# Streams' states loaded ahead into the ring for unsplit weights, and the first MLP pair's differences formed in the mixer's last round

## The chip, the cores and the metric

One core of a Trainium2 chip runs the whole kernel. The metric is device time in microseconds (us), lower is better. The core's engines are TensorE (PE in the rows; PEld is its loading of stationary operands), VectorE (DVE), ScalarE (ACT), GpSimd (POOL) and SyncE (SP), which here issues every DMA, in the order of its queue.

## The reference, cut to what matters

One inference step of one layer, in fp32, for a prompt of 16 meta and 2048 tokens and for 8 running streams of 16 new tokens each, width 1024.

```python
q, k, v, gate, ga, gb = split(rms_norm(x, g_pre) @ w_in)     # 1024 -> 3072
q, k = rope(q), rope(k) * HEAD_DIM ** -0.5                   # 4 heads of 128
scores = einsum('bihd,bjhd->bhij', q, k) * d_intra           # retention, chunks of 64
out    = scores @ v + (q @ S) * d_in                         # S: carried state, 128 x 128
S_new  = S * exp(lg * L) + einsum('bjhd,bjhe,hj->bhde', k, v, d_out)
ret    = group_norm(out) * silu(gate)
conv   = silu(layer_norm(depthwise_conv31(ga * sigmoid(gb))))
x = x + rms_norm(concat(ret, conv) @ w_out)
x = x + rms_norm(square(relu(rms_norm(x) @ w_mlp_in)) @ w_mlp_out)
```

For a running stream S is an input (`state_ret`, 8 streams x 4 heads x 128 x 128) and S_new an output (`o_ss` in the kernel).

## The kernel before, in words

Tokens lie along the free axis, features along the 128 partitions. Each fp32 product is made of three matmuls: both operands are split into a high and a low part, and `mm3` adds low x high, high x low and high x high (L514 to L516). A split is one ScalarE copy and one subtraction on DVE or POOL (L383, L384).

**Mixer.** The tokens form six groups of 2 or 3 blocks of 128 (`LAY`); group `SG` = 3 holds two prompt blocks and one block with the 8 streams. For each group in turn the projection `w_in`, four heads (`head`, names `tk`, `up`, `us`, `os`, `ob`, `ot`), the convolution with its norm (`conv_norm`, names `cv`, `mu`, `z`, `acc`, `cacc`, `st`, `rb`) and the output projection `w_out` (result `yo`, stored in `yscr`) run as generators that are advanced between the main matmuls `mm`. Weights are read unsplit once (`raw`, a ring of 5 tiles of 128x512 in the mixer, `RB`), split, stored to DRAM (`wkeep_in`, `wkeep_out`) and from then on read as `whi` and `wlo` through a ring of nine. The normalized mixer output of all groups is stored in DRAM in pieces of 128 rows (`hd`).

**Sampled streams.** In group 3 each head goes through the 8 streams two at a time: load of two states into `sst` (a ring of two tiles, L1038), product with the masked queries (`os`, L1040), decay and addition of the new outer products `us` in place (DVE, L1042), store to `o_ss` (L1044).

**Column sums.** `rstd_bcast` (L487) sums the squares over the partitions: for each block of 128 tokens the squares are the stationary operand and a 128x128 tile of ones is the moving one; only column 0 of the result is read. A call leaves two records in the profile.

**MLP.** The columns are taken in three groups `G` of two halves (384, 384 and 320 columns each). For each, seven products replace eight in the manner of Strassen, so seven combined operands `P1` to `P7` (names `op`) are made of the four quarters of `hd`: with b11, b12 the two column halves of the upper rows and b21, b22 of the lower, the operands are b11, b21, b22 and the differences b12 - b11 (P5), b22 - P5 (P6), b22 - b12 (P7) and b21 - P6 (P4). For G = 1 and 2 `differences` forms the four on POOL while the MLP of the pair before runs, stores them in `td`, and `reload` brings them in and splits them. For G = 0 `make_h2` does it on DVE after the mixer's last head, while TensorE still makes the last `w_out` products: it loads a 128x768 piece with both halves (`st`, L616), subtracts (L622) and splits (L384). Layer 2's seven products (`SEVEN`, `plan`) are the same in both kernels.

The order within each engine is settled when the program is built, by a scheduler that plays the program through; SyncE's queue is in that order too.

Of the kernel before, what the change touches and what calls it, by code (L numbers as in the profile page):

```python
# [12 lines left out]
F32 = mybir.dt.float32  # L13
# [3 lines left out]
ALU = mybir.AluOpType  # L17
# [3 lines left out]
P = 128  # L21
D_MODEL, SEQ, N_META, PAST_LEN = 1024, 2048, 16, 512
NS, SL = 8, 16
# [146 lines left out]
def build(nc, T):  # L170
    lg = _log_gamma()
    with tile.TileContext(nc, schedule_with_timeline_sim=True) as tc, ExitStack() as top:
# [306 lines left out]
        def rstd_bcast(acc, W, n):  # L479
# [6 lines left out]
            for b, s in enumerate(starts):  # L486
                nc.tensor.matmul(ps[:, b, :], acc[:, s:s + P], ones, start=True, stop=True)  # L487
# [108 lines left out]
        OPS = (P1, P2, P6, P5, P7, P3, P4)  # L596
# [3 lines left out]
        td = [None] + [dram.tile([4, 4, P, n], F32, name=f"td{n}") for n in NH2[1:]]  # L600
# [6 lines left out]

        def make_h2(G, which, eng, put):

            n = NH2[G]  # L610
            need = {P1: (0,), P2: (1,), P3: (1,), P5: (0,), P6: (0, 1), P7: (0, 1), P4: (0, 1)}
            for k in range(4):
                bs = {}
                for r in sorted({r for x in which for r in need[x]}):
                    t = st_tile()[:, :2 * n]
                    nc.sync.dma_start(t, hd[G][k + 4 * r])  # L616
                    bs[r, 0], bs[r, 1] = t[:, :n], t[:, n:]
                yield

                def diff(a, b):  # L620
                    t = s_tile(n)
                    eng.tensor_tensor(out=t, in0=a, in1=b, op=ALU.subtract)  # L622
                    return t

                parts = {P1: bs.get((0, 0)), P2: bs.get((1, 0)), P3: bs.get((1, 1))}
                if {P4, P5, P6} & set(which):
                    parts[P5] = diff(bs[0, 1], bs[0, 0])
                if {P4, P6} & set(which):
                    parts[P6] = diff(bs[1, 1], parts[P5])
                for x in which:  # L630
                    if x == P7:
                        parts[x] = diff(bs[1, 1], bs[0, 1])
                    if x == P4:
                        parts[x] = diff(bs[1, 0], parts[P6])
                    yield from put(x, k, parts[x])

        def put_home(G, eng):
            def put(x, k, part):
                t = hops[G, x] if k else home(G, x)
                split(part, t[:, k], t[:, 4 + k], eng)  # L640
                if k == 3:
                    h2_made.add((G, x))
                yield
            return put

        def differences(G):

            n = NH2[G]
            for k in range(4):
# [7 lines left out]
                for i in range(4):  # L657
# [5 lines left out]
                    ts.append(t)  # L663
                    yield
# [294 lines left out]
        def head_tail(gi, h, kr, qr, vf):  # L959
# [4 lines left out]
            sblk = slice(nb * P, N)  # L964

# [58 lines left out]
            if smp:  # L1024
                osm = auxp.tile([P, 512], F32, tag="aux", name="os")[:, :P]
                for s0 in range(0, NS, 4):
# [8 lines left out]
                    for s1 in (0, 2):  # L1035
                        s = s0 + s1
                        sst = tp.tile([P, 2, P], F32, tag="sst", name="sst", bufs=2)
                        nc.sync.dma_start(sst, T["state"][h][:, s:s + 2, :])  # L1038
                        for i in range(2):
                            nc.tensor.matmul(osm, qdm[:, (s + i) * (P - SL):(s + i) * (P - SL) + P], sst[:, i],  # L1040
                                             start=(s + i == 0), stop=False)
                        nc.vector.scalar_tensor_tensor(out=sst, in0=sst, scalar=float(np.exp(lg[h] * SL)),  # L1042
                                                       in1=us[:, s1:s1 + 2], op0=ALU.mult, op1=ALU.add)
                        nc.sync.dma_start(T["o_ss"][h][:, s:s + 2, :], sst)  # L1044
# [54 lines left out]
        for gi in range(len(LAY)):  # L1099
# [24 lines left out]
            if gi == LAST:  # L1124
                rate["norm"] = 2
            for h, t in late(gi):
                head_unit(gi, h, t)
# [354 lines left out]
```

## Time and profile before

| | |
|---|---|
| median of 3 runs | 2417.91 us (2410.08 to 2423.68) |
| profiled execution | 2409.09 us |
| its span | 2407.3 us |
| mean granted clock of TensorE | 0.987 |

The span is the time from the first to the last recorded instruction, the profiled execution the device's time for the same run. The granted clock is a share of full speed: 1 means 2.4 GHz all along.

### The profile page before, as it was taken

The page shows a single profiled execution, that of the slowest core. Times are in us where ns is not written, and L with a number is a line of the kernel's source. Part 1 is how long each engine was busy: PE and PEld are TensorE (multiplying, and loading weights), DVE is VectorE, ACT ScalarE, POOL GpSimd, SP SyncE. Part 2 cuts the span into 40 slices and gives each one's busy share as a digit, 9 for nine tenths or more (in the row PEclk, how much of TensorE's full clock was granted, in tenths as well). Part 3 has the DMA queues.
Part 4 walks back from the last instruction along what each step waited for, and adds up shares of the span by engine and source line. Part 5 has one row for each costly group of instructions (what it writes and reads, how often), then busy time and mean ns, then how long its engine had stood idle before and what let it go on. Part 6 is the DMA issues. An engine that isn't in the chain of part 4 may idle for free. (4 is left out here: it accounts for less than half of the span.)

```text
span 2407.3 us, 41425 instructions
## 1 busy us (share of the span) xinstructions
PE 2312.4 (96%) x14250; PEld 2277.5 (95%) x14250; DVE 1708.5 (71%) x3704; ACT 1005.1 (42%) x2240; POOL 1470.6 (61%) x1532
## 2 busy tenths in 40 slices
PE   8898999998899998999999999999899999999997
PEld 7898999998899998999999999999899999999997
DVE  8999897896997965546543347678776676666666
ACT  5534334123223133544434445344444443444442
POOL 6847232131133113978888776687897747888874
PEclk9999999999999999999999999999999999999998
DMA  8887787897688778858896557676765567565562
GB/s 316 284 313 273 269 291 265 243 329 275 204 275 285 242 251 322 281 203 291 279 321 228 188 203 253 229 237 216 259 215 166 167 222 260 181 203 175 190 216 95
DMA packets 246338, 584.55 MB, mean 243 GB/s; under 512 B 31984, under 2 KB 106480, under 8 KB 246128
## 3 DMA queue, kind: packets, MB, share of 16 engines
q1 hardware_dynamic: 246128, 581.92, 71.2%
q8 instruction: 112, 1.84, 0.3%
q14 instruction: 98, 0.80, 0.1%
HBM read 445.20 MB, written 136.61 MB: 242 GB/s over the span
## 5 line engine op out<-in xcount | busy, mean ns | idle before, releaser
L1227 PE MATMUL mm<-op,wp 128*128 128x384 f32 (+1 forms) x1344 | 441.9, 329 | 13.3 <-DMA wp<-wprod 12.7
L1229 PE MATMUL mm<-op,wp 128*128 128x384 f32 (+1 forms) x1344 | 439.3, 327 | 1.5 <-POOL wp L322 1.5
L1228 PE MATMUL mm<-op,wp 128*128 128x384 f32 (+1 forms) x1344 | 439.8, 327 | 0.0
L835 DVE SCALAR_TENSOR_TENSOR cv<-ext,par,cv 128x384 f32<-128x384 f32 (+1 forms) x720 | 381.8, 571 | 2.0
L514 PE MATMUL mm<-hhi,whi 128*128 128x384 f32 (+2 forms) x992 | 332.6, 336 | 17.4 <-ACT hhi L731 5.4
L516 PE MATMUL mm<-hhi,wlo 128*128 128x384 f32 (+2 forms) x992 | 331.9, 336 | 7.3 <-DMA wlo<-wkeep_in 3.1
L515 PE MATMUL mm<-hlo,whi 128*128 128x384 f32 (+2 forms) x992 | 331.3, 334 | 0.3
L283 POOL TENSOR_TENSOR wlo<-raw,whi 128x512 fp32r<-128x512 f32 x180 | 239.0, 1347 | 127.2 <-ACT whi L282 52.2
L1320 DVE TENSOR_TENSOR ya<-l2y,ya 128x384 f32<-128x384 f32 (+1 forms) x384 | 194.6, 519 | 117.1 <-PE l2y L1317 116.3
L1227 PEld LDWEIGHTS mm<-op,wp 128*128 128x128 f32 x1344 | 252.9, 188 | 21.8 <-DMA wp<-wprod 7.8
L1229 PEld LDWEIGHTS mm<-op,wp 128*128 128x128 f32 x1344 | 252.9, 188 | 1.9 <-POOL wp L322 1.7
L1228 PEld LDWEIGHTS mm<-op,wp 128*128 128x128 f32 x1344 | 253.0, 188 | 0.1
L356 POOL TENSOR_TENSOR wq<-raw,wq 128x256 fp32r<-128x256 f32 x240 | 183.1, 776 | 58.7 <-ACT wq L355 58.0
L514 PEld LDWEIGHTS mm<-hhi,whi 128*128 128x128 f32 x992 | 191.5, 193 | 19.8 <-ACT hhi L731 5.6
L384 POOL TENSOR_TENSOR fo<-c,fo 128x384 fp32r<-128x384 f32 (+1 forms) x168 | 166.2, 990 | 65.3 <-ACT fo L383 64.1
L516 PEld LDWEIGHTS mm<-hhi,wlo 128*128 128x128 f32 x992 | 190.7, 193 | 10.2 <-DMA wlo<-wkeep_in 3.8
L515 PEld LDWEIGHTS mm<-hlo,whi 128*128 128x128 f32 x992 | 191.0, 193 | 1.5 <-DVE hlo L732 1.1
L1320 DVE TENSOR_TENSOR ya<-l2w,ya 128x384 f32<-128x384 f32 (+1 forms) x288 | 143.1, 517 | 19.3 <-PE l2w L1317 16.7
L1241 DVE TENSOR_TENSOR c<-mm,sn 128x384 f32<-128x384 f32 (+1 forms) x144 | 76.5, 532 | 112.7 <-PE mm L1229 74.5
L322 POOL TENSOR_TENSOR wp<-raw,wp 128x512 fp32r<-128x512 f32 x96 | 126.9, 1327 | 43.9 <-ACT wp L321 31.5
L882 POOL TENSOR_TENSOR sw<-sw,sin 128x384 f32<-128x384 f32 (+2 forms) x48 | 48.3, 1006 | 171.0 <-ACT sw L879 168.5
L282 ACT ACTIVATE whi<-raw 128x512 fp32r<-128x512 f32 x192 | 112.9, 623 | 85.4 <-DMA raw<-w_in 19.0
(261 smaller groups left out, 6292.2 us busy)
## 6 DMA issues: line engine op xcount, KB each, us to landing
wp<-wprod SPq DMA_DIRECT2D x224, 512.0 KB, 3.9
raw<-w SPq DMA_DIRECT2D x256, 256.0 KB, 3.8
wprod<-wp SPq DMA_DIRECT2D x112, 512.0 KB, 3.9
whi<-wkeep_in SPq DMA_DIRECT2D x108, 512.0 KB, 6.2
wlo<-wkeep_in SPq DMA_DIRECT2D x108, 512.0 KB, 5.3
raw<-w_in SPq DMA_DIRECT2D x72, 256.0 KB, 5.6
whi<-wkeep_out SPq DMA_DIRECT2D x36, 512.0 KB, 6.0
wlo<-wkeep_out SPq DMA_DIRECT2D x36, 512.0 KB, 5.7
```

Of the source, the lines that this page charges most:

```text
L283: (nc.vector if i < 24 and i % 4 == 0 else nc.gpsimd).tensor_tensor(out=lo[:, c], in0=raw, in1=hi[:, c].bitcast(F32), op=ALU.subtract)
L322: tt(out=op[:, H:], in0=src, in1=op[:, :H].bitcast(F32), op=ALU.subtract)
L356: nc.gpsimd.tensor_tensor(out=op[:, o + H:o + 2 * H], in0=src, in1=op[:, o:o + H].bitcast(F32), op=ALU.subtract)
L384: (eng or nc.gpsimd).tensor_tensor(out=lo, in0=src, in1=hi.bitcast(F32), op=ALU.subtract)
L514: nc.tensor.matmul(ps, whi(k), ahi(k), start=(k == 0), stop=False)
L515: nc.tensor.matmul(ps, whi(k), alo(k), start=False, stop=False)
L516: nc.tensor.matmul(ps, wlo(k), ahi(k), start=False, stop=(k == nk - 1))
L835: nc.vector.scalar_tensor_tensor(out=o, in0=src(t), scalar=wt, in1=o, op0=ALU.mult, op1=ALU.add)
L1227: nc.tensor.matmul(ps, hi, ops[:, k, :n], start=start, stop=False, skip_group_check=not first)
L1228: nc.tensor.matmul(ps, hi, ops[:, 4 + k, :n], start=False, stop=False, skip_group_check=not first)
L1229: nc.tensor.matmul(ps, lo, ops[:, k, :n], start=False, stop=(k == 3), skip_group_check=not first)
L1320: last_y[0] = nc.vector.tensor_tensor(out=y, in0=ps, in1=y, op=ALU.add)
```

## The change

It consists of three edits. The states of a head's eight streams are loaded at the beginning of `head`, four streams at a time, into tiles of the `raw` ring, and are used from there; product, update and store take four streams in one go. The column sums use one column of the ones. The four differences of G = 0 are formed on POOL by a new generator `first_differences`, queued behind `mlp_in` in the last round of the mixer, with pieces of `hd` loaded into the two halves of one tile `df`; they are stored in a `td` of their own, and `make_h2` gives way to `reload`, which `differences` of G = 1 and 2 already use. (`reload` loads a k pair, 128x2x384, of one operand, from `hd` for P1, P2, P3 and from `td` for the others, and splits it, half on DVE and half on POOL for G = 0.)

```diff
--- before.py
+++ after.py
@@ -484,7 +484,7 @@
             nb = len(starts)
             ps = auxp.tile([P, 4, P], F32, tag="aux", name="st")
             for b, s in enumerate(starts):
-                nc.tensor.matmul(ps[:, b, :], acc[:, s:s + P], ones, start=True, stop=True)
+                nc.tensor.matmul(ps[:, b, :1], acc[:, s:s + P], ones[:, :1], start=True, stop=True)
             y = rsqrt_small(ps[:, :nb, 0], nb, n)
             dg = spool.tile([P, NM // P, P], F32, tag="dg", name="dg", bufs=1)
             for b in range(nb):
@@ -593,55 +593,16 @@
                 yield
 
 
-        OPS = (P1, P2, P6, P5, P7, P3, P4)
         HOME = {P1: "hhi", P2: "hlo", P6: "chi", P5: "clo", P7: "x", P3: "hhi", P4: "hlo"}
         hops, h2_made = {}, set()
 
-        td = [None] + [dram.tile([4, 4, P, n], F32, name=f"td{n}") for n in NH2[1:]]
+        td = [dram.tile([4, 4, P, n], F32, name=f"td{G}") for G, n in enumerate(NH2)]
 
         def home(G, x):
             pool = {"h": hp, "c": catp, "x": xp}[HOME[x][0]]
             t = pool.tile([P, 8, NM if pool is catp else WM], F32R, tag=HOME[x], name=f"op{x}")
             hops[G, x] = t[:, :, :NH2[G]]
             return hops[G, x]
-
-        def make_h2(G, which, eng, put):
-
-            n = NH2[G]
-            need = {P1: (0,), P2: (1,), P3: (1,), P5: (0,), P6: (0, 1), P7: (0, 1), P4: (0, 1)}
-            for k in range(4):
-                bs = {}
-                for r in sorted({r for x in which for r in need[x]}):
-                    t = st_tile()[:, :2 * n]
-                    nc.sync.dma_start(t, hd[G][k + 4 * r])
-                    bs[r, 0], bs[r, 1] = t[:, :n], t[:, n:]
-                yield
-
-                def diff(a, b):
-                    t = s_tile(n)
-                    eng.tensor_tensor(out=t, in0=a, in1=b, op=ALU.subtract)
-                    return t
-
-                parts = {P1: bs.get((0, 0)), P2: bs.get((1, 0)), P3: bs.get((1, 1))}
-                if {P4, P5, P6} & set(which):
-                    parts[P5] = diff(bs[0, 1], bs[0, 0])
-                if {P4, P6} & set(which):
-                    parts[P6] = diff(bs[1, 1], parts[P5])
-                for x in which:
-                    if x == P7:
-                        parts[x] = diff(bs[1, 1], bs[0, 1])
-                    if x == P4:
-                        parts[x] = diff(bs[1, 0], parts[P6])
-                    yield from put(x, k, parts[x])
-
-        def put_home(G, eng):
-            def put(x, k, part):
-                t = hops[G, x] if k else home(G, x)
-                split(part, t[:, k], t[:, 4 + k], eng)
-                if k == 3:
-                    h2_made.add((G, x))
-                yield
-            return put
 
         def differences(G):
 
@@ -661,6 +622,21 @@
                     nc.gpsimd.tensor_tensor(out=t, in0=x, in1=y, op=ALU.subtract)
                     nc.sync.dma_start(td[G][i, k], t)
                     ts.append(t)
+                    yield
+
+        def first_differences():
+
+            n = NH2[0]
+            t = xp.tile([P, KT * WM], F32, tag="x", name="df")
+            for k in range(4):
+                b11, b12, b21, b22 = (t[:, (k % 2 * 4 + i) * WM:(k % 2 * 4 + i) * WM + n] for i in range(4))
+                for r, pair in ((0, (b11, b12)), (1, (b21, b22))):
+                    for c in range(2):
+                        nc.sync.dma_start(pair[c], hd[0][k + 4 * r][:, c * n:(c + 1) * n])
+                yield
+                for i, (o, x, y) in enumerate(((b11, b12, b11), (b12, b22, b12), (b22, b22, b11), (b21, b21, b22))):
+                    nc.gpsimd.tensor_tensor(out=o, in0=x, in1=y, op=ALU.subtract)
+                    nc.sync.dma_start(td[0][(0, 2, 1, 3)[i], k], o)
                     yield
 
         def reload(G, x):
@@ -962,6 +938,12 @@
             nt = nb + smp
             blk = [slice(b * P, (b + 1) * P) for b in range(nt)]
             sblk = slice(nb * P, N)
+            ssts = []
+            for s0 in range(0, NS if smp else 0, 4):
+
+                ssts.append(rawps[0].tile([P, 512], F32, tag="raw", name="sst", bufs=RB[0]).rearrange(
+                    "p (s d) -> p s d", s=4))
+                nc.sync.dma_start(ssts[-1], T["state"][h][:, s0:s0 + 4, :])
 
             tk = auxp.tile([P, 512], F32, tag="aux", name="tk")
             tv = auxp.tile([P, 512], F32, tag="aux", name="tv") if m else None
@@ -1032,16 +1014,13 @@
                                           in1=smask[:, s:s + 2].unsqueeze(2).to_broadcast([P, 2, P]), op=ALU.mult)
                         for i in range(2):
                             nc.tensor.matmul(us[:, s - s0 + i], ks[:, i], vt[:, sblk], start=True, stop=True)
-                    for s1 in (0, 2):
-                        s = s0 + s1
-                        sst = tp.tile([P, 2, P], F32, tag="sst", name="sst", bufs=2)
-                        nc.sync.dma_start(sst, T["state"][h][:, s:s + 2, :])
-                        for i in range(2):
-                            nc.tensor.matmul(osm, qdm[:, (s + i) * (P - SL):(s + i) * (P - SL) + P], sst[:, i],
-                                             start=(s + i == 0), stop=False)
-                        nc.vector.scalar_tensor_tensor(out=sst, in0=sst, scalar=float(np.exp(lg[h] * SL)),
-                                                       in1=us[:, s1:s1 + 2], op0=ALU.mult, op1=ALU.add)
-                        nc.sync.dma_start(T["o_ss"][h][:, s:s + 2, :], sst)
+                    sst = ssts[s0 // 4]
+                    for i in range(4):
+                        nc.tensor.matmul(osm, qdm[:, (s0 + i) * (P - SL):(s0 + i) * (P - SL) + P], sst[:, i],
+                                         start=(s0 + i == 0), stop=False)
+                    nc.vector.scalar_tensor_tensor(out=sst, in0=sst, scalar=float(np.exp(lg[h] * SL)), in1=us,
+                                                   op0=ALU.mult, op1=ALU.add)
+                    nc.sync.dma_start(T["o_ss"][h][:, s0:s0 + 4, :], sst)
                 nc.tensor.matmul(osm, sd[:, sblk], vt[:, sblk], start=False, stop=True)
             yield
 
@@ -1123,6 +1102,7 @@
             queues["conv"].append(conv_norm(gi))
             if gi == LAST:
                 rate["norm"] = 2
+                queues["mlp"].append(first_differences())
             for h, t in late(gi):
                 head_unit(gi, h, t)
             if gi < LAST:
@@ -1145,12 +1125,12 @@
         RB.append(8)
         stqs.append(ep(tc.tile_pool(name="stq", bufs=3)))
         rate["norm"] = 4
-        queues["norm"].append(make_h2(0, (P1, P2, P7), nc.vector, put_home(0, nc.vector)))
+        queues["norm"] += [reload(0, x) for x in (P1, P2, P7)]
         out_units(LAST - 1, range(SPLIT, 8))
-        queues["norm"].append(make_h2(0, (P6, P5), nc.vector, put_home(0, nc.vector)))
+        queues["norm"] += [reload(0, x) for x in (P6, P5)]
         mlp_on.append(1)
         out_units(LAST)
-        queues["norm"].append(make_h2(0, (P3, P4), nc.vector, put_home(0, nc.vector)))
+        queues["norm"] += [reload(0, x) for x in (P3, P4)]
 
         def prologue(G):
             for gi in FG[G]:
```

Line numbers in the rows of the kernel after differ by the length of what was taken out: `sst` is loaded at L946, `o_ss` stored at L1023, `df` loaded at L635 and stored at L639, `reload` loads at L653, and the `z` chain stands at L839 to L846.

SyncE's queue at the streams' last heads, before. `sst` are the states, `yscr_101` the `w_out` product of group 2, `wlo` and `whi` weights.

```order
L549 DMA s<-yscr_101 128x384 x8
L257 DMA wlo<-wkeep_in 128x1024
L256 DMA whi<-wkeep_in 128x1024
L549 DMA s<-yscr_101 128x384
L554 DMA s<-x 128x384
L549 DMA s<-yscr_101 128x384
L554 DMA s<-x 128x384
L549 DMA s<-yscr_101 128x384
L1044 DMA o_ss<-sst 128x256 x2
L1038 DMA sst<-state 128x256 x2
L1044 DMA o_ss<-sst 128x256 x2
L1038 DMA sst<-state 128x256 x2
```

SyncE's queue while the last first-use pieces of `w_out` are read for group 1 (`yscr_100` is its output), after: here the first of the states stand now.

```order
L281 DMA raw<-w_out 128x512
L377 DMA wkeep_out<-wlo 128x1024
L946 DMA sst<-state 128x512
L257 DMA wlo<-wkeep_out 128x1024
L1073 DMA yscr_100<-yo 128x384
L375 DMA wkeep_out<-whi 128x1024
L256 DMA whi<-wkeep_out 128x1024
L1073 DMA yscr_100<-yo 128x384
L946 DMA sst<-state 128x512
L377 DMA wkeep_out<-wlo 128x1024
L946 DMA sst<-state 128x512
L257 DMA wlo<-wkeep_out 128x1024
```

The load of a state stood directly behind the store of another; now three of the loads (the other two of the first five follow within eight rows) stand behind the last first-use load of `w_out`, and the first `o_ss` follows more than a hundred rows later.

SyncE's queue in the mixer's last round, before (`hd` is stored by `mlp_in` of group 2, `cos` and `sin` are tables).

```order
L256 DMA whi<-wkeep_in 128x1024
L592 DMA hd_108<-s 128x384 x2
L257 DMA wlo<-wkeep_in 128x1024
L592 DMA hd_108<-s 128x384
L256 DMA whi<-wkeep_in 128x1024
L757 DMA cos<-cos 128x384
L758 DMA sin<-sin 128x384
L257 DMA wlo<-wkeep_in 128x1024
L256 DMA whi<-wkeep_in 128x1024
L257 DMA wlo<-wkeep_in 128x1024
L256 DMA whi<-wkeep_in 128x1024
```

The same place, after.

```order
L257 DMA wlo<-wkeep_in 128x1024
L256 DMA whi<-wkeep_in 128x1024
L639 DMA td_111<-df 128x384 x3
L257 DMA wlo<-wkeep_in 128x1024
L256 DMA whi<-wkeep_in 128x1024
L639 DMA td_111<-df 128x384
L635 DMA df<-hd_108 128x384 x2
L257 DMA wlo<-wkeep_in 128x1024
L635 DMA df<-hd_108 128x384
L256 DMA whi<-wkeep_in 128x1024
L635 DMA df<-hd_108 128x384 x2
L257 DMA wlo<-wkeep_in 128x1024
```

Weights followed on weights; now loads of `df` and stores of `td` stand between them.

SyncE's queue in the passage to the MLP, before (`raw<-w` are the first MLP weights, `yscr_103` and `yscr_104` the last two groups' output).

```order
L616 DMA st<-hd_108 128x768 x3
L257 DMA wlo<-wkeep_out 128x1024
L256 DMA whi<-wkeep_out 128x1024
L1094 DMA yscr_103<-yo 128x384
L616 DMA st<-hd_108 128x768 x7
L304 DMA raw<-w 128x512 x2
L257 DMA wlo<-wkeep_out 128x1024
L256 DMA whi<-wkeep_out 128x1024
L1094 DMA yscr_104<-yo 128x384 x3
L257 DMA wlo<-wkeep_out 128x1024
L256 DMA whi<-wkeep_out 128x1024
```

The same place, after.

```order
L1073 DMA yscr_103<-yo 128x384
L653 DMA st<-td_111 128x2x384
L653 DMA st<-hd_108 128x2x384 x2
L304 DMA raw<-w 128x512 x3
L257 DMA wlo<-wkeep_out 128x1024
L1073 DMA yscr_104<-yo 128x384 x3
L256 DMA whi<-wkeep_out 128x1024
L257 DMA wlo<-wkeep_out 128x1024
L256 DMA whi<-wkeep_out 128x1024
```

Seven loads of pieces of `hd` stood ahead of a `wlo`; now there are three smaller loads, and the three stores of `yscr_104` have come ahead of a `whi`.

DVE's rows in the passage, before (`z` is the last convolution's output on its way to `chi`, `op` are the operands).

```order
L384 TENSOR_TENSOR op_11114<-s,op_11114 128x384
L622 TENSOR_TENSOR s<-st,s 128x384
L863 TENSOR_TENSOR z_10044<-z_10044,rb 128x384
L863 TENSOR_TENSOR z_10046<-z_10046,rb 128x384
L863 TENSOR_TENSOR z_10622<-z_10622,rb 128x384
L863 TENSOR_TENSOR z_10624<-z_10624,rb 128x384
L622 TENSOR_TENSOR s<-st 128x384
L384 TENSOR_TENSOR op_11111<-s,op_11111 128x384
L867 TENSOR_SCALAR z_10044<-z_10044,par 128x384
L867 TENSOR_SCALAR z_10046<-z_10046,par 128x384
L622 TENSOR_TENSOR s<-st,s 128x384
L384 TENSOR_TENSOR op_11114<-s,op_11114 128x384
```

The same place, after.

```order
L1041 SCALAR_TENSOR_TENSOR nm<-mv,nw_10841 128x3
L839 TENSOR_TENSOR z_10013<-z_10013,rb 128x384
L839 TENSOR_TENSOR z_10015<-z_10015,rb 128x384
L839 TENSOR_TENSOR z_10614<-z_10614,rb 128x384
L839 TENSOR_TENSOR z_10616<-z_10616,rb 128x384
L384 TENSOR_TENSOR op_11109<-st,op_11109 128x384 x2
L384 TENSOR_TENSOR op_11154<-st,op_11154 128x384
L843 TENSOR_SCALAR z_10013<-z_10013,par 128x384
L843 TENSOR_SCALAR z_10015<-z_10015,par 128x384
L846 TENSOR_TENSOR z_10013<-z_10013,csg 128x384
L846 TENSOR_TENSOR z_10015<-z_10015,csg 128x384
```

The differences of L622 are gone from among the steps of `z`; three splits of operands stand between two of its steps.

## Rows read from the trace of the kernel before

**Rows 1.** Windows: busy us of each engine, granted clock, DMA share.
```profile
core 0: us, PE busy (x) PEld busy (x) DVE busy (x) ACT busy (x) POOL busy (x), PEclk, DMA share, GB/s
580.00:620.00 40.00, 26.39 (x135) 24.52 (x135) 30.78 (x86) 17.80 (x39) 9.39 (x11) 0.83 0.56 182
650.00:900.00 250.00, 247.01 (x1605) 245.93 (x1604) 203.67 (x506) 74.69 (x163) 57.76 (x55) 0.99 0.77 262
920.00:950.00 30.00, 21.94 (x98) 19.33 (x97) 18.18 (x29) 11.35 (x22) 11.42 (x9) 0.83 0.80 276
```
**Rows 2.** Waits of TensorE, whole program: total us, times, longest.
```profile
PE os L1040 <- DMA sst<-state: 5.9, 2, 4.4
```
**Rows 3.** Waits, 578 to 625 us.
```profile
PE os L1040 <- DMA sst<-state: 4.4, 1, 4.4
...
PE mm L514 <- DVE gs L953: 3.3, 1, 3.3
...
PE st L487 <- DVE cacc L509: 2.0, 1, 2.0
PE ot L1072 <- ACT on L1067: 1.9, 1, 1.9
...
PE os L1040 <- DVE S L1019: 1.2, 1, 1.2
```
**Rows 4.** Timeline of SyncE: start us, us until all were issued.
```profile
585.82 14.22 SPq L549 DMA_DIRECT2D s<-yscr  x8
...
606.78 0.91 SPq L1044 DMA_DIRECT2D o_ss<-sst  x2
610.52 0.81 SPq L1038 DMA_DIRECT2D sst<-state  x2
```
**Rows 5.** Timeline of TensorE: start us, us.
```profile
616.27 0.52 PE L515 MATMUL mm<-hlo,whi 128*128 128x384 f32 x1
616.59 0.52 PE L516 MATMUL mm<-hhi,wlo 128*128 128x384 f32 x1
...
619.33 0.33 PE L514 MATMUL mm<-hhi,whi 128*128 128x384 f32 x1
619.50 0.33 PE L515 MATMUL mm<-hlo,whi 128*128 128x384 f32 x1
```
**Rows 6.** Waits of TensorE, 900 to 1000 us.
```profile
PE mm L516 <- DMA wlo<-wkeep_out: 3.6, 1, 3.6
PE mm L514 <- ACT chi L383: 3.0, 2, 2.8
...
PE mm L515 <- POOL clo L384: 1.2, 3, 0.7
```
**Rows 7.** Timeline of SyncE in the passage.
```profile
922.79 14.95 SPq L616 DMA_DIRECT2D st<-hd  x7
...
938.74 0.42 SPq L257 DMA_DIRECT2D wlo<-wkeep_out  x1
```
**Rows 8.** Groups of DVE: count, busy us, mean ns, idle before.
```profile
L622 DVE TENSOR_TENSOR s<-st,s 128x384 f32<-128x384 f32 x12 | 10.4, 865 | 19.5 <-DMA st<-hd 19.3
L622 DVE TENSOR_TENSOR s<-st 128x384 f32<-128x384 f32 x12 | 9.7, 806 | 3.9 <-DMA st<-hd 3.9
```
**Rows 9.** Timeline of TensorE, column sums and their neighbours.
```profile
906.99 0.83 PE L487 MATMUL st<-cst,cacc 128*128 128x128 f32 x6
907.66 0.49 PE L1072 MATMUL ot<-cst,on 128*128 128x128 f32 x3
907.98 0.39 PE L1050 MATMUL ob<-S,qd 128*128 128x128 f32 x2
```
**Rows 10.** Groups of POOL: `differences` of the later pairs.
```profile
L661 POOL TENSOR_TENSOR s<-st,s 128x384 f32<-128x384 f32 (+1 forms) x16 | 15.4, 962 | 0.0
```
**Rows 11.** Timelines of DVE and POOL around 754 us.
```profile
753.57 1.28 POOL L882 TENSOR_TENSOR sw<-sw,sin 128x384 f32<-128x384 f32 x1 [1.01 <-ACT sw L879]
...
753.90 1.37 DVE L883 TENSOR_TENSOR kr<-kr,sw 128x384 f32<-128x384 f32 x1
756.30 0.56 DVE L883 TENSOR_TENSOR qr<-qr,sw 128x384 f32<-128x384 f32 x1
```

## The prediction

> **What bounds the kernel now.** I read the windows first. Between 650 and 900 us, a plain stretch of the mixer, TensorE is busy for 247.01 of 250 us [rows 1]: nothing that another engine saves there can show. The stretch 580 to 620 us is different: 26.39 of 40 us, at a mean granted clock of 0.83 [rows 1]. The kernel's other thin place that the diff touches is 920 to 950 us, 21.94 of 30 us, also at 0.83 [rows 1]. The first is the group with the sampled streams, the second the passage from the mixer to the first MLP pair. So the price of the change is read from these two.
>
> The waits of TensorE say what ended last. Over the whole program `os` waits 5.9 us for the states `sst` [rows 2], in two waits, the longer 4.4 us. Within 578 to 625 us four more waits stand beside it: `gs` 3.3, the column sums for `cacc` 2.0, `on` 1.9, `S` 1.2 us [rows 3], 8.4 us together. In SyncE's own row the cause of the 4.4 us is plain: two stores of `sst` are issued at 606.78, the loads that refill the same two buffers go out only at 610.52, 3.74 us later [rows 4], since a buffer must be stored before it is loaded; and ahead of that the queue stood 14.22 us in front of eight loads of `yscr` [rows 4]. A standstill also costs after its end: from 616.27 to 616.59 one matmul of 384 columns follows the next after 0.32 us, from 619.33 to 619.50 after 0.17 us [rows 5]. The slower pace is the 1.2 GHz level, the faster the 2.4 GHz one. About ten matmuls ran at the slow pace after the 4.4 us wait, and as many after the 3.3 us one, 0.15 us more each: 1.5 us a stretch.
>
> In the passage TensorE waits 3.6 us for `wlo`, 3.0 for `chi` and 1.2 for `clo` [rows 6]. The 3.6 us come from SyncE again: it stood 14.95 us at seven loads `st<-hd`, whose ring was full, and the `wlo` that TensorE needed was issued behind them at 938.74 [rows 7].
>
> **The change, part by part.** All sums are against the profiled execution, 2409.1 us (span 2407.3 and 1.8 us around it). The median of the runs is 2417.9, a factor of 1.0037 above it, with which I end.
>
> *States.* Sixteen loads of 128 KB in a ring of two become eight of 256 KB in the five raw buffers. In the new order five go out in the round of group 1, some hundred rows of SyncE's queue ahead of the first `o_ss`; behind the last first-use load of `w_out` nothing else wants these buffers until the MLP. So the store no longer stands between a state and its reload, and the 5.9 us go in full. DVE's update of `sst` no longer stands in its queue for `os`, and the second head's `os` moves ahead by some sixty main matmuls, so part of the four other waits goes: DVE's chain stood for the same states and then ran late to `gs`, `S` and the sums. I take two thirds of 8.4, 5.6 us; all of it is one bound, nothing the other, since the order does not show how long the chains themselves are. Two slow stretches of 1.5 us go with the waits: 3.0. Sum **14.5 us**; bounds 0 (another wait takes the place) and 17.3.
>
> *Passage.* Before, 24 loads of 384 KB bring both halves of `hd`, DVE makes 24 differences (10.4 + 9.7 = 20.1 us of its time [rows 8]) and 28 splits. Now 14 loads bring finished operands, DVE makes no difference, and 14 of the splits go to POOL. Ten loads fewer in a ring of the same size means that the wait in front of the `wlo` loses its cause: I take the 3.6 us and the slow stretch behind it (1.5) in full. `chi` waits for DVE's normalization chain `z`, in which differences stood before and fewer operations stand now; but two op splits stand behind the four `z` and before the next step, so I take half of 3.0 + 1.2 and of a stretch, 2.85. Sum **8.0 us**. The upper bound is 10.8 (3.6 + 5.7 and the 1.5). The lower is −5: of the new queue, `whi` of the next block stands behind three stores of `yscr`, which wait for `yo`; a like queue error cost 3.6 + 1.5 above.
>
> *One column in the sums.* 94 matmul records lose 127 of their 128 columns. Six of them take from 906.99 to 907.66, 0.112 us each, and three `ot` of the same shape from 907.66 to 907.98, 0.107 each [rows 9]. Each has its own weights of 128 columns to load, which the change leaves. So the time between two is taken to be that of the load, and only 0.112 − 0.107 is saved: 94 × 0.005 = **0.5 us**. Bounds: 0, and the whole pass, 94 × 0.112 = 10.5.
> The Trainium skill, TensorE: Matmul & The Clock Gate, section LDWEIGHTS, says that a load of the stationary operand takes its time by the 128 columns of the array and not by what streams behind it. By it the sum would be that same half microsecond and not the 10.5 of the pass; the rows above, in which two kinds of matmul come at nearly one pace, agree, and none has one column.
>
> *Differences in the last round.* What leaves the passage is paid here: 16 subtractions on POOL, 16 loads of 192 KB, 16 stores, 32 more issues on SyncE. Sixteen such subtractions stand in the trace at 962 ns, 15.4 us in all [rows 10]. They lie between 750 and 800 us or thereabouts, inside the stretch in which POOL works 57.76 of 250 us and the DMA engines 0.77 of the time [rows 1]: POOL's idle time hides them. If that cover were gone they would cost up to 15.4. TensorE's cover against SyncE is the ring of weights ahead: the 14.22 us standstill above left no wait for weights in the waits of that stretch, the 14.95 us one left 3.6 [rows 3, 4, 6, 7]. Issues of some 0.4 us in between are nothing to that. I put **−1 us**; bounds 0 and −10.
>
> The title's seven products in layer 2 remove and add no instruction: the table of products is not in the diff and TensorE's rows in the MLP stay as they were. Nought.
>
> Sum: 14.5 + 8.0 + 0.5 − 1 = 22.0. 2409.1 − 22.0 = 2387.1, times 1.0037 is **2396 us**.
>
> **Rivals.**
> *Only the direct wait returns.* TensorE's other waits in the sampled group are chains of ScalarE and DVE (`gs`, `on`, the sums) which no edit shortens, and in the passage the wait moves from `wlo` to `whi` or `chi`. For it: four of the five waits of [rows 3] name no state. Against it: DVE stood behind `os` in that stretch. Then 5.9 + 0.5 − 1 = 5.4 remain: 2403.7, as a median 2412, no change.
> *POOL slows DVE in the passage.* The 14 splits go to POOL while DVE has two-input operations. One such on DVE took 1.37 us beside POOL's `sw`, and 0.56 us when POOL rested [rows 11]. Fourteen splits and about six `z` operations at 0.81 more are 16 us of DVE in a passage of thirty, and `chi` comes no sooner: the 8.0 go. Then 14.5 + 0.5 − 1 = 14.0 remain: 2395.1, as a median 2404. Against it: DVE has lost 20.1 us of differences, more than that.
> The Trainium skill, SBUF — State Buffer, section Who interferes with whom, says that a VectorE operation with two inputs from SBUF and a GpSimd operation block one another for a whole instruction; the two rows above agree. It speaks against sharing the splits between the two, and by it the gain of the passage would be nought.
> *Slower: the queue in the last round.* SyncE issues in order. The stores `td0` wait for POOL, the loads into the same half tile wait for the stores. If each of eight pairs of loads waits 3.74 us for a store, as `sst` did [rows 4], and all of the 15.4 us of subtractions are waited for, SyncE stands 8 × 3.74 + 15.4 = 45.3 us, and the mixer's weights queue behind it. Were none of this covered: 2409.1 − 22.0 + 45.3 = 2432.4, as a median 2441. For the whole to be slower at all it must cost TensorE more than 23 us net, for slower by 0.5% more than 34; with the 14 us that a standstill has free, nearly every wait would have to fall in one stretch. The order spreads them over four rounds of loads with weights between.
>
> **How the numbers follow.** Forecast 0.52, only the direct wait 0.26, POOL against DVE 0.15, slower queue 0.07. Low end: the upper bounds of states and passage and most of that of the one column, a gain of 36, 2373, as a median 2382. High end: the first rival, 2412, and 2 us for bounds of its own terms: 2414. The likeliest case alone spans 2385 to 2405. Half a percent, 12 us, is about what a measurement of this kernel tells from no change; faster is below 2406, slower above 2430. The forecast lies below 2406 with nearly all of its chance (0.49), the POOL rival with somewhat over half (0.09), the first rival with a sixth (0.04): 0.62 faster. Slower: 0.06, most of the last case. The rest, 0.32, is no change.
>
> **What would show it.** Right: no wait of `os` for `sst`; in the sampled group's stretch TensorE's busy share up and the granted clock above 0.83; no wait for `wlo` in the passage and `st<-hd` standing far less than 14.95 us; sums of one column at about 0.11 us apiece; TensorE as busy as now while POOL subtracts. Wrong: waits for `gs`, `on`, `S` as long as now (states mis-sized); a wait for `whi` or `chi` in the passage; waits for `whi` or `wlo` in the last round, with SyncE standing at `df` or `td0`; one-column sums well under 0.1 us, which would make the gain larger.

## The result, and the profile after

The changed kernel takes 2395.4 us (median of 6 runs, 2391.0 to 2404.1), the kernel before in the same comparison 2416.1 us (6 runs). The ratio is 0.9919, with a 95% interval of 0.9903 to 0.9935: 19.6 us less, 16 to 23 by the interval. The forecast was 2396 us. The profiled execution took 2391.47 us, its span is 2389.3.

The windows of the kernel after, with the columns of [rows 1]:

```profile
580.00:620.00 40.00, 38.34 (x257) 38.12 (x257) 39.22 (x94) 17.31 (x40) 12.85 (x13) 1.00 0.75 253
650.00:900.00 250.00, 246.89 (x1596) 245.76 (x1595) 201.27 (x502) 78.44 (x172) 78.42 (x75) 0.99 0.86 296
920.00:950.00 30.00, 25.61 (x145) 24.65 (x143) 8.84 (x4) 9.46 (x20) 19.44 (x16) 0.99 0.98 371
```

The sampled group's stretch is full now: TensorE is busy for 38.34 us where it was 26.39, at a clock of 1.00 where it was 0.83. In the mixer's last rounds POOL works 20.7 us more (78.42 against 57.76) and the DMA share rises from 0.77 to 0.86, and TensorE is as busy as before.

All waits of TensorE in the kernel after from 500 to 650 us (total, times, longest):

```profile
PE tk L951 <- DVE sst L1021: 1.7, 1, 1.7
PE ob L1029 <- DVE sst L1021: 0.9, 1, 0.9
PE rb L495 <- DVE dg L491: 0.2, 1, 0.2
PE mm L910 <- DMA wlo<-wkeep_in: 0.2, 1, 0.2
```

3.0 us together. Before it was 17.0: the 5.9 of [rows 2], the 8.4 of the four waits beside it in [rows 3], and 2.7 in two more that the prediction did not count:

```profile
PE mm L933 <- DVE kr L881: 1.9, 1, 1.9
PE us L1034 <- DVE z L863: 0.8, 1, 0.8
```

No wait for `sst` from memory is left, and none of the other six either; the 1.7 and 0.9 us for DVE's update of `sst` are new. SyncE's timeline shows how early the states come: the first one is loaded 183 us before the first `o_ss`.

```profile
328.66 0.42 SPq L946 DMA_DIRECT2D sst<-state  x1
...
511.99 0.34 SPq L1023 DMA_DIRECT2D o_ss<-sst  x1
```

The passage, 890 to 960 us, again all waits of TensorE:

```profile
PE mm L1207 <- DVE c L1221: 2.9, 1, 2.9
PE mm L516 <- DMA wlo<-wkeep_out: 1.8, 2, 1.4
PE mm L515 <- POOL clo L384: 1.5, 3, 0.7
PE mm L1207 <- ACT sn L1216: 0.6, 1, 0.6
PE mm L514 <- ACT chi L383: 0.3, 1, 0.3
```

Against [rows 6], `wlo` fell from 3.6 to 1.8, `chi` from 3.0 to 0.3; `clo` stayed (1.2, now 1.5), and the first MLP products wait 2.9 us for `c`, a sum that DVE forms from a product (0.2 before). In SyncE's queue the standstill at the pieces of `hd` is gone, but not the one in front of the `wlo`:

```profile
902.79 0.37 SPq L653 DMA_DIRECT2D st<-td  x1
904.09 1.66 SPq L653 DMA_DIRECT2D st<-hd  x2
913.85 1.30 SPq L304 DMA_DIRECT2D raw<-w  x3
915.24 0.38 SPq L257 DMA_DIRECT2D wlo<-wkeep_out  x1
```

From 905.75 to 913.85 SyncE issues nothing: it stands at the first MLP weights (`raw<-w`) until DVE's work on `z` and POOL's on `clo` is done. SyncE's two longest waits from 904 to 916 us:

```profile
SPq L304 <- DVE z L843: 5.1, 1, 5.1
SPq L304 <- POOL clo L384: 2.9, 1, 2.9
```

So the 14.95 us of [rows 7] became 8.1, and the two waits for `wlo` are for the tiles issued next behind them, at 915.24 and 917.86. (The loads at L653 are fewer, not smaller than those before: 128x2x384 is as many bytes as 128x768.)

**By stages.** The main matmuls come in nearly the same order in all these kernels. So the same matmul can be looked up in two timelines of TensorE, and the difference of its start is what was gained or lost up to there. The table gives it against the profiled execution of before (minus is earlier), at the matmuls that started there at 560 us (ahead of the knot in the sampled group), 640 (behind it), 740 and 800 (about the last round's differences), 890 and 990 (ahead of and behind the passage) and 2385; each is the median over the matmuls of the 9 us around it. It is one execution each, and the experiments of the next section stand in it too. Where the order differs, an entry depends on how the matmuls are paired: by their plain count three entries move by 2 us (e9 at 640, -23.3; e7 and e12 at 990, -24.3 and -27.4), the others by up to 1.

```
                                              560    640    740    800    890    990   2385
one column alone (e2)                        -0.5    0.1   -3.1   -2.8   -3.0   -4.4    3.4
differences alone (e3)                       -0.9   -3.6   -0.1   -0.1   -0.1   -3.6   -2.4
four streams, one buffer (e4)                -3.5   -8.8  -11.7   -7.4   -7.4   -9.3   -4.6
states alone (e1)                             4.3  -12.8  -19.5  -19.9  -19.4  -17.5  -13.4
states and one column (e6)                    3.8  -18.7  -19.3  -19.2  -19.3  -17.9   -9.7
the changed kernel, first profile             4.9  -17.0  -17.5  -17.3  -17.5  -22.1  -18.1
the changed kernel, second profile (e5)       4.1  -17.4  -17.6  -14.2  -13.8  -19.6  -17.6
changed, all first splits on DVE (e7)         0.1  -22.5  -23.1  -17.3  -17.4  -26.4  -20.8
changed, all first splits on POOL (e8)        6.4  -13.5  -16.0   -9.5   -9.5  -12.9   -5.9
states, one column, last round's work (e9)   -1.2  -25.2  -26.4  -20.3  -20.4  -20.0  -13.1
e9 without the subtractions (e10)             4.5  -18.1  -20.8  -19.3  -19.6  -18.1  -14.2
changed, subtractions on DVE (e11)            2.9  -20.2  -21.8  -21.3  -21.3  -23.7  -15.8
both on DVE (e12)                             4.7  -17.6  -19.9  -20.0  -19.5  -29.4  -18.0
```

From 560 to 640 every kernel with the early states gains 17 to 24 us. Part of this are small matmuls that now run ahead of 560 and make most of these kernels late there (from 500 to 560 the changed kernel has 96 beside the main ones, the kernel before 62; from 560 to 640 it is 127 and 154). What they have gained in all stands at 740: 16 to 26 us, and 19.5 for the states alone. From 890 to 990 every kernel with the new passage gains 2 to 10 (2 to 8 by the plain count), while those with early states and the old passage lose 0 to 2 there (e9 loses 0.4). From 740 to 800 the 4.3 us that e4 loses are for the most part small matmuls again: 101 fall there, against 74 in the kernel before and 80 to 83 in those with early states. (The profile of e4, 2404.5 us, lies 7 us below the median of its runs.) From 990 to 2385 all come out later than the profiled execution of before, also the one with a single column, by 1 to 11 us: that execution had a short MLP. It lies 7 us below the median of its own runs, and what looks like a loss there is no part of the change.

### The profile page after: what moved, and what is told of

Read it like the earlier page. It is cut to its first block, busy times and chain, and to the rows that moved or that the text cites. A ratio compares the mean times of both kernels' runs of the same rounds, so it can differ in the third digit from the quotient of the medians.

```text
span 2389.3 us, 41429 instructions
## 1 busy us (share of the span) xinstructions
PE 2302.5 (96%) x14250; PEld 2267.5 (95%) x14250; DVE 1697.1 (71%) x3658; ACT 1002.7 (42%) x2240; POOL 1498.5 (63%) x1562
```

## The experiments

Twelve kernels were run. Their ratios are to the kernel before on the same chip, with 95% intervals. The first four make one edit each in the kernel before.

**States alone (e1).** `head` as in the changed kernel, nothing else of the diff.

> The kernel before with the states edit alone. Theory (the store that stands before each reload, and SyncE's queue, held the whole sampled group up): 16 to 21 us less than before (ratio 0.991 to 0.9935), no wait of os for sst, the stretch 580 to 620 us at a granted clock near 1.00. Rival (only the direct wait goes, the other chains stay): 5 to 8 us less, and waits for gs, on and the sums still there.

0.9918 (0.9905 to 0.9932): 19.8 us less. This edit alone gives what all three give together. TensorE's waits from 500 to 650 us, and its stretch of the sampled group with the columns of [rows 1]:

```profile
PE ot L1076 <- ACT on L1071: 1.8, 1, 1.8
PE tk L976 <- DVE sst L1046: 1.6, 1, 1.6
PE sc L995 <- ACT kd L986: 0.8, 1, 0.8
PE mm L514 <- DVE kr L881: 0.2, 1, 0.2
580.00:620.00 40.00, 37.56 (x237) 37.14 (x236) 37.14 (x92) 15.72 (x37) 11.03 (x13) 0.91 0.65 214
```

The rival, that only the direct wait goes, is out: of the other waits one for `on` is left. The clock is 0.91 there, not near 1.00 as expected; a short slow stretch remains in this profile.

**One column alone (e2).**

```diff
-                nc.tensor.matmul(ps[:, b, :], acc[:, s:s + P], ones, start=True, stop=True)
+                nc.tensor.matmul(ps[:, b, :1], acc[:, s:s + P], ones[:, :1], start=True, stop=True)
```

> The kernel before with one column in the sums and nothing else. Theory (the load of the stationary operand sets the pace): within 1 us of before, six records still 0.11 us apart. Rival (the moving columns set it): up to 10 us less, records well under 0.1 us apart.

0.9995 (0.9984 to 1.0007), no difference that can be told. In the changed kernel's timeline of TensorE, six such records and what follows them:

```profile
737.75 0.73 PE L487 MATMUL st<-cst,cacc 128*128 128x1 f32 x6
738.34 0.42 PE L515 MATMUL mm<-hlo,whi 128*128 128x384 f32 x1
```

0.59 us for six, 0.098 apart, where [rows 9] have 0.112. One column is a little faster than taken, by this pace 94 x 0.014 = 1.3 us in all, but far from a pass that costs nothing.

**Differences alone (e3).** `first_differences` and `reload` for the first pair in the kernel before; states and sums as they were.

> The kernel before with the first pair's differences formed in the mixer's last round and reloaded, states and sums as before. Theory: 4 to 8 us less, all of it in the passage; the last round no slower than 1 us. Rival (the last round pays through SyncE's queue, or POOL beside DVE eats the passage's gain): no less than before.

0.9970 (0.9955 to 0.9984): 7.2 us less. The table has 3.5 of it in the passage of the one profiled execution, and nothing lost in the last round (740 to 800).

**Four streams at a time in one buffer (e4).** The load stays where the states are used, with as many bytes of buffer as before:

```diff
-                    for s1 in (0, 2):
-                        s = s0 + s1
-                        sst = tp.tile([P, 2, P], F32, tag="sst", name="sst", bufs=2)
-                        nc.sync.dma_start(sst, T["state"][h][:, s:s + 2, :])
+                    sst = tp.tile([P, 512], F32, tag="sst", name="sst", bufs=1).rearrange(
+                        "p (s d) -> p s d", s=4)
+                    nc.sync.dma_start(sst, T["state"][h][:, s0:s0 + 4, :])
...
```

> The kernel before with states loaded, used and stored four streams at a time, but in one buffer of the size that the two of before had together. Theory (what matters is that a load does not wait for a store): no less than before, up to 15 us more, with more waits of os for sst. Rival (half as many transfers and updates are what helps): nearly as much less as with the states edit alone, 10 us or more.

0.9988 (0.9974 to 1.0001): far from the states edit, and no slower than before. So half as many transfers are not what helps; but more waits of `os` for `sst`, which the theory expected, did not come either. TensorE's waits from 580 to 620 us:

```profile
PE mm L514 <- ACT sg L785: 4.8, 1, 4.8
PE ot L1071 <- ACT on L1066: 3.2, 1, 3.2
PE sc L988 <- ACT rn L1073: 1.3, 1, 1.3
PE rb L495 <- DVE dg L491: 0.9, 1, 0.9
PE ob L1049 <- DVE sst L1041: 0.7, 1, 0.7
```

No wait of `os` for `sst` is among them, though here too the load went out only behind a store (issued at 606.55 us, landed at 609.49): TensorE stood for `sg` until 607.92 and had main matmuls to do behind it. The stretch is nearly as empty as before (28.98 of 40 us busy, clock 0.74). So the hole does not go with the wait that names it. The rest I read from the order: in e4 the last `os` of the second head stands behind 3061 of the program's main matmuls (3059 before) and the first of the third head behind 3096 in both. Only 35 of them (37 before) lie between, and what hangs on the late `os`, `ob`, `on`, `ot` and the `z` chain, falls into this short piece of the queue. In the changed kernel the two stand behind 2959 and 3090, 131 apart. What the waits then name, `sst`, `gs` or `sg`, is who came last. No run moved the `os` without the loads, so that the place in the order makes the hole is argued, not shown; shown is that the early loads close it (e1).

The next four compare with the changed kernel on one chip.

**The changed kernel again (e5), and without the differences (e6).** e6 has `head` and the one column of the changed kernel and `make_h2` of before.

> The changed kernel as it is, as the measure for the next three on the same chip: ratio 0.990 to 0.9935.

> The changed kernel with the edit of the differences undone (states and one column stay). Theory A (the passage's gain, 3 us per thousand when it was made alone, comes on top): 4 to 8 us slower than the changed kernel. Theory B (the states' gain and the passage's do not add: what the passage saves is given back behind it or in the last round): within 2 us of the changed kernel.

0.9927 (0.9907 to 0.9947) and 0.9928 (0.9910 to 0.9947); medians 2393.7 and 2394.2. The medians go with theory B: the 7 us that the differences gave alone are not seen on top of the states, within the 5 us either way that the runs leave. The table shows where some of them can go. The passage does gain (890 to 990: 4.6 and 5.8 us in the two profiles of the changed kernel, against a loss of 1.4 in e6). But from 740 to 800 the second profile loses 3.4 us, e7 5.8 and e8 6.5, and e6 nothing. (In e7 to e9, with waits of 3.0 to 3.5 us there, the granted clock falls to 0.97 as well, so the slow pace behind the wait is part of the loss; in e5 it stays at 1.00.) In the timelines of e5, of DVE first, and then of POOL and of TensorE:

```profile
740.68 0.15 DVE L452 TENSOR_SCALAR nw<-st 128x3 int32<-128x3 int32 x1
740.86 0.16 DVE L454 TENSOR_TENSOR nw<-nw 128x3 f32<-128x3 f32 x1
741.06 0.16 DVE L455 SCALAR_TENSOR_TENSOR nw<-nw,st 128x3 f32<-128x3 f32 x1
741.25 0.68 DVE L456 SCALAR_TENSOR_TENSOR nw<-nw,nw 128x3 f32<-128x3 f32 x1
741.97 0.94 DVE L457 TENSOR_TENSOR nw<-nw 128x3 f32<-128x3 f32 x1
742.95 0.16 DVE L458 SCALAR_TENSOR_TENSOR nw<-nw,st 128x3 f32<-128x3 f32 x1
743.14 0.74 DVE L460 SCALAR_TENSOR_TENSOR nw<-nw 128x3 f32<-128x3 f32 x1
743.92 0.92 DVE L462 SCALAR_TENSOR_TENSOR nw<-nw,nw 128x3 f32<-128x3 f32 x1
744.87 1.49 DVE L491 TENSOR_SCALAR dg<-cst,nw 128x128 f32<-128x128 f32 x3
```
```profile
741.88 4.01 POOL L638 TENSOR_TENSOR df<-df 128x384 f32<-128x384 f32 x4
```
```profile
746.02 0.94 PE L495 MATMUL rb<-dg,cst 128*128 128x128 f32 x6 [1.97 <-DVE dg L491]
```

Eight operations on 128 x 3 numbers, the reciprocal root of a norm, run one behind the other. The first three take 0.15 to 0.16 us. Of the next five four take 0.68 to 0.94, L456 beside POOL's `qd` (so too in the first profile, 0.69) and the others beside its subtractions; the one that does not, L458, reads `st`, which lies in PSUM, and L455, as quick beside `qd`, does too. Each of the four slow ones ends 0.02 us after an operation of POOL. The three `dg` behind them, with one tile as input, took 1.49 us against 0.68 in the first profile. So the chain with its `dg` ends some 3 us late, and `rb` waits for it. In the first profile of the changed kernel the same four subtractions began at 743.59, after the chain had ended (its `dg` began at 743.12):

```profile
743.59 4.13 POOL L638 TENSOR_TENSOR df<-df 128x384 f32<-128x384 f32 x4 [1.30 <-DMA df<-hd]
```

and nothing was lost. There POOL had waited 1.30 us for a transfer; so little decides. That fits the Trainium skill, SBUF — State Buffer, section Who interferes with whom: a VectorE operation with two inputs from SBUF and a GpSimd operation that reads SBUF exclude each other for a whole instruction, and with one input there is no conflict outside of special modes. The four slow operations have two inputs from SBUF and agree, and so does L458 with an operand in PSUM. `dg` reads one tile and was slowed too; whether it ran in one of the special modes no run here tells.

**All of the first pair's splits on one engine (e7, e8).** In `reload`, for G = 0:

```diff
-                split(ld[k // 2][:, k % 2], t[:, k], t[:, 4 + k], nc.vector if k % 2 else nc.gpsimd)
+                split(ld[k // 2][:, k % 2], t[:, k], t[:, 4 + k], nc.vector if k % 2 or G == 0 else nc.gpsimd)
```

e7 so; e8 with `nc.vector if k % 2 and G else nc.gpsimd`.

> The changed kernel with all 28 splits of the first pair on DVE, none on POOL. If POOL beside DVE slows the passage: 2 to 6 us faster than the changed kernel, chi and clo waits shorter. If DVE's free time is what matters: up to 3 us slower, z later. If neither: the same within 1 us.

> The changed kernel with all 28 splits of the first pair on POOL. If splits in front of the z chain hold chi up: 1 to 4 us faster than the changed kernel. If POOL becomes late for clo and for wp instead: 2 to 8 us slower, with waits of TensorE for clo and wp. If neither: the same within 1 us.

e7 0.9913 (0.9894 to 0.9932), e8 0.9943 (0.9922 to 0.9964); e5 lies between. Each interval takes in the 0.9927 of e5, so by time neither is told from it; e8 is told from e7, 7.6 us slower by the means of six runs each, give or take 5. By the table the passage gains 9.0 us in e7 (6.9 by the plain count), 5.8 in e5 and 3.4 in e8. In e8 the waits for `chi` (4.0 us) and `wlo` (3.0) are back:

```profile
PE mm L514 <- ACT chi L383: 4.0, 1, 4.0
PE mm L516 <- DMA wlo<-wkeep_out: 3.0, 1, 3.0
PE mm L515 <- POOL clo L384: 1.4, 1, 1.4
```

DVE's steps of `z` on the way to `chi` (890 to 935 us; count, busy us, mean ns), in e5, e7 and e8:

```profile
L846 DVE TENSOR_TENSOR z<-z,csg 128x384 f32<-128x384 f32 x3 | 2.3, 779 | 0.0
L846 DVE TENSOR_TENSOR z<-z,csg 128x384 f32<-128x384 f32 x3 | 2.3, 779 | 0.0
L846 DVE TENSOR_TENSOR z<-z,csg 128x384 f32<-128x384 f32 x3 | 3.7, 1240 | 0.1
```

With all 28 splits POOL slows the chain that `chi` waits for; with 14, as in the changed kernel, these steps are as quick as with none. It is one profile each.

The last four, on a third chip, take the last round apart.

**The last round's work without its use (e9), and without the subtractions (e10).** e6 with `first_differences` added, which stores in a `td0` that nobody reads, since `make_h2` still forms the operands; e10 then leaves this line out, so that what it stores are the loaded pieces:

```diff
-                    nc.gpsimd.tensor_tensor(out=o, in0=x, in1=y, op=ALU.subtract)
```

> The kernel with states and one column, to which the last round's work is added (16 loads, 16 subtractions on POOL, 16 stores) while the passage stays as before and makes its operands itself, so the stored differences are read by nobody. Theory (the states' gain and the passage's do not add because POOL's subtractions fall beside DVE's short reciprocal-root chain in the last round): 2 to 6 us slower than states and one column alone, so a ratio near 0.995 to before, with a wait of rb for dg of 2 to 3 us. Rival (the last round hides the work; the passage itself gives less when the states are early): within 1.5 us of states and one column alone, 0.9928.

> The same with the 16 subtractions left out; the loads and stores of the last round remain and what is stored is the loaded pieces, read by nobody. Theory (POOL beside DVE): within 1.5 us of states and one column alone, no wait of rb for dg in the last round. Rival (queue and transfers): as slow as with the subtractions.

e9 0.9932 (0.9916 to 0.9948), e10 0.9917 (0.9904 to 0.9931). By time e9 came out where the rival put it, 1 us above e6 (0.9928, on another chip), not at the theory's 0.995; against e10 on its own chip it is 2.7 us slower by the medians, less than can be told. The traces show what the theory said: from 740 to 800 e9 loses 6.1 us and e10 1.5. TensorE's waits from 730 to 745 us, in e9 and then in e10:

```profile
PE rb L495 <- DVE dg L491: 2.1, 2, 1.6
```
```profile
PE st L487 <- DVE cacc L509: 0.4, 1, 0.4
```

With the 32 transfers alone 1.5 us are lost there; the rest comes with the subtractions, in one profile each.

**The subtractions on DVE (e11), and the splits too (e12).**

```diff
-                    nc.gpsimd.tensor_tensor(out=o, in0=x, in1=y, op=ALU.subtract)
+                    nc.vector.tensor_tensor(out=o, in0=x, in1=y, op=ALU.subtract)
```

e12 adds the edit of e7.

> The changed kernel with the 16 subtractions of the last round on DVE in place of POOL. Theory: DVE's chain keeps its pace, no wait of rb for dg; 0 to 4 us faster than the changed kernel. Rival (DVE is the fuller engine in the last round, its 16 x 0.55 us delay the chains): 1 to 5 us slower.

> The changed kernel with the 16 subtractions on DVE and all splits of the first pair on DVE. If both hold (POOL off the first pair altogether): 4 to 8 us faster than the changed kernel, near 0.990 to before. If not: no better than with the splits alone, 0.9913.

e11 0.9905 (0.9888 to 0.9922), e12 0.9898 (0.9885 to 0.9910). From 740 to 800 they lose 0.5 us and nothing, so DVE has room for the 16 subtractions (16 in 8.7 us), and no wait of `rb` for `dg` over 0.2 us is left. In the passage of e11's profile one wait ate most of the gain, for the split of an operand on DVE:

```profile
PE mm L1208 <- DVE op L384: 7.7, 1, 7.7
```

In e12 it is gone, and the passage gains 9.9 us (7.9 by the plain count). With 2391.0 us (4 runs) against 2414.8 for the kernel before, 24 us less, e12 has the lowest ratio of all; the changed kernel did not run on that chip, its intervals elsewhere (to 0.9903 at the low end) overlap with that of e12, so a lead of some 5 us over it is likely and not proved.

## Why the prediction was right, and where not

The time was right almost to the microsecond, and that is in part luck: the states gave more than their term, and the passage's gain, right by itself, did not show on top of them.

- **States, 14.5 us.** The mechanism was right, the size too small: 19.8 by the timed runs of e1, and its profile is 19.5 us ahead at 740. The direct wait of 5.9 went, the slow pace behind the waits was about as taken (21 matmuls of 384 columns took 0.47 us or more between 560 and 650 us in before, one in after; 21 x 0.15 = 3.2 against 3.0). The step that failed is "two thirds of 8.4": all of the four went, and with them the 1.9 for `kr` and the 0.8 for `z`, which had no term. Over 500 to 650 us TensorE waited 17.0 us before and 3.0 after, 14.0 less, and 14.0 + 3.2 = 17.2; the rest is not accounted for row by row. The other waits were for the most part not chains that stay when the states come early, as e1 shows; that they came through the place that the scheduler gave to what hangs on the states is the reading of e4's order.
- **Passage, 8.0 us.** Right in size by time when it is made alone (7.2), but "the wait in front of the `wlo` loads loses its cause" was wrong: SyncE now stands 8.1 us at the first MLP weights, in front of the same `wlo`. The wait for `chi` nearly went, of which I had taken half; half of the wait for `wlo` stayed, which I had taken in full; and a wait for `c` came, which I had not named. The bound of −5 for `whi` behind `yscr` was not touched: no wait for `whi` stands in the passage.
- **One column, 0.5 us.** Right in kind: 1.3 by the pace of the rows, and no difference that the runs can tell.
- **Last round, −1 us.** This step failed by the traces. "POOL's idle time hides them" looked at POOL alone. The subtractions have room on POOL, but they can fall beside DVE's chain: in four of the five profiles with early states and subtractions on POOL they hit it, and the stretch lost 3.4 to 6.5 us. I had this contention among the rivals, with its row [rows 11], but only for the passage. With late states (e3) the last round lost nothing in the one profile that there is. So up to 6.5 us of the passage's gain can go there; in the first profile of the changed kernel none went, and by time the loss is not told (e9 against e10). Why the two gains do not add is shown in part only.
- **Queue in the last round.** This rival is out: with the transfers alone, in e10, the stretch lost 1.5 us, and no wait for weights stood in it.
- **Only the direct wait returns.** This rival is out by e1. **POOL slows DVE in the passage:** not in the changed kernel, whose steps of `z` are as quick as those of e7; seen in e8, with all 28 splits on POOL, which is also slower than e7 by time.
- **The factor of 1.0037** was needed: the profiled execution of before lay below the median, and in every other profile the MLP took longer than in it.

Not settled: why the gains of the states and of the passage do not add; whether the differences on POOL, on top of the states, are worth nothing or up to 4 us either way, and whether e12 leads the changed kernel by the whole 5 us.

## What to carry to other kernels

When several waits of different names stand close together, look for one buffer or load on which all may depend, and price the whole hole in the busy time, not the wait that names it. Before work is put into POOL's idle time, look whether DVE runs a chain of short operations there that TensorE waits for; here the same 16 subtractions on DVE cost at most 0.5 us in their stretch. Make each part of a change alone and then leave each part out: gains that are real by themselves need not add.

## What the hardware showed that was not expected

Operations on 128 x 3 numbers, 0.16 us each, took 0.68 to 0.94 us beside POOL's operations of 1.0 us (e5), 4 to 6 times as long. A subtraction that costs POOL 1.02 us (16 in 16.2) costs DVE 0.55 (16 in 8.7, e11).
